# A decoder block on one core: the first products in a written order, two elementwise steps on other engines

## The chip, the core and the metric

The kernel runs on one core of one Trainium2 chip. Its engines are TensorE (PE in the profile; PEld is its loading of weights), VectorE (DVE), ScalarE (ACT), GpSimd (POOL) and SyncE (SP, which issues the transfers here). Each has a queue of its own and works it off in order; they wait for each other by semaphores. The metric is the device time of one execution in microseconds (us), the median of several runs.

## What is computed

One layer of a hybrid decoder for 256 tokens of width 1024, in float32: a norm, one combined projection, attention and a gated scan (SSD) beside each other, a mixed output, and a second part (PEER) that scores 16384 single-neuron experts. With one block of 256 keys the attention is plain causal attention with slopes. Cut to what the change touches:

```python
h = rms_norm(x, norm1_g)
q, k, v, z, xbc, dt_raw, g_attn, g_ssd = split(h @ w_in)
q, k = rms_norm(q, q_norm_g), rms_norm(k, k_norm_g)
s = q @ k.T * 64 ** -0.5 - slopes * dist            # per head, causal
p = softmax(s)
attn = p @ v
xs, bm, cm = split(silu(conv(xbc)))
acum = cumsum(dt * -exp(a_log))
lmat = exp(where(causal, acum[t] - acum[s], -inf))  # per scan head
y = (cm @ bm.T * lmat) @ (xs * dt)                  # 8 groups of 4 scan heads
x = x + (sigmoid(g_attn) * (attn @ w_attn_o) + sigmoid(g_ssd) * (norm(y) @ w_ssd_o)) @ w_out
x = x + peer(rms_norm(x, norm2_g))
```

## The kernel before

**Products.** Every float32 matrix is split into a high part that TensorE can take in one pass (type fp32r) and the rest. A product is the sum of three: high x high (hh), the low part of the activations with the high part of the weights (lh), and high with low (hl). `hTh` and `hTl` are the parts of the normed, transposed activations, `wh` and `wl` those of the weights.

**Weights.** `load_raw` (line 110) loads tiles of 128 x 1024 floats, 512 KB each, into three buffers `wr`, in the order in which they are used; `ahead` (line 116) keeps five loads and three splits ahead of the product. A split is one copy on ScalarE (`wh`, line 128) and one subtraction for `wl`, on VectorE (line 138) or, for every third or fourth tile, on GpSimd (line 133). A buffer `wr` is free for the next load when `wl` is made.

**Stages.** For each of 8 groups g: the columns of q and k (`psqk`), of v for two groups (`psv`), of xs (`psxs`), of B and C (`psbc`), of z (`psz`). Each such product is 48 matmuls of 256 columns on two weight tiles. `product_N` (line 198) has tokens as rows, `product_T` (line 165) as columns. Between the matmuls `tick` (line 151) calls generators that emit the other work in small steps: `decay` once (it makes `dt`, line 344, with the product `psdt` of 24 matmuls and the small transposes `psdtn`), and for each group `attention` (line 424), `conv`, `zgate` and `ssd` (line 556). So the order of TensorE is that of the program's text from the first group on. Other engines' instructions are put in order by a scheduler from its own estimates; `K` (line 80) keeps an instruction in program order instead, and is used for the start alone.

**The start.** SP loads the first 128 rows of x, the gains, weight tile 0, the other 128 rows, and tiles 1 and 2. TensorE runs 13 products of zeros (`pz`, line 282). `norm_T` (line 238) is a generator for each half of the rows: `rnm` (mean square plus epsilon, VectorE), `rn` (power -0.5, GpSimd), `xn` (rows scaled, VectorE), four and four transposes to `ptx`, then `hTh` (ScalarE, line 267) and `hTl` (VectorE, line 271) in pieces of 128 columns. The squares of the first half are summed by ScalarE, those of the second by VectorE (line 294). The tuple `START` (line 30) says in which order the two halves and the first splits are emitted. The first psqk uses `product_half` with `late`, which sorts the terms of a weight tile by hh, lh, hl.

**In attention**, after the exponentials `p` and their sums, VectorE makes the reciprocals `rs` (line 481), GpSimd scales the rows of p with two instructions per head (line 483), TensorE transposes them (`pp`, line 488). **In ssd**, `seg` makes the exponents `e` (VectorE, lines 583 and 584), and `damp` (line 586) takes the exponential and multiplies it with the masked scores `cbm` to `m`: two of four on VectorE, two on GpSimd. TensorE multiplies m with xs (`py`, line 619); `y`, `yT` and `yl` are VectorE's steps behind it.

Of the kernel before, what the change touches and what calls it, by code (L numbers as in the profile page):

```python
# [9 lines left out]
F32 = mybir.dt.float32  # L10
# [19 lines left out]
START = (0, 1, 2, 0, 1, 2, 1)  # L30
# [31 lines left out]
def tile_hybrid_block(ctx: ExitStack, tc: tile.TileContext, x, n1g, wblk, wdt, qkg, cw, cb, dtb,  # L62
# [135 lines left out]
    def product_N(ps, xh, xl, late=False):  # L198

        w = natural_w()  # L200
        for tt in range(2):
            product_half(ps, tt, w, xh, xl, late)

    def rstd_of(pool, ss, n, inv, name):
# [3 lines left out]
        state["pow"] = nc.gpsimd.tensor_tensor(q, r, neghalf[:, :n], op=OP.pow)  # L208
# [8 lines left out]
    with tc.tile_pool(name="pa", bufs=1) as pa, ExitStack() as ctx2:  # L217
# [20 lines left out]
        def norm_T(pool, tt, ss, gain, dh, dl, tag, row=False):  # L238
# [3 lines left out]
            if row and tt == 0:  # L242
                yield
            t = slice(128 * tt, 128 * tt + 128)
            pts = []
            for f in range(2):
                xn = pool.tile([128, 512], F32, name="xn", tag="w512", bufs=W512)
                c = slice(512 * f, 512 * f + 512)
                if row:
                    state["xn"] = V.scalar_tensor_tensor(xn, xt[:, tt, c], r, gain[:, c], op0=OP.mult, op1=OP.mult)  # L250
                else:
                    K(V.tensor_scalar(xn, xt[:, tt, c], r, None, op0=OP.mult))
# [5 lines left out]
            for f in range(2):  # L258
                if row:
                    k = slice(4 * f, 4 * f + 4)  # L260
                    state["behind"] = (
                        A.activation(dh[:, k, t], pts[f], AF.Copy),
                        V.tensor_tensor(dl[:, k, t], pts[f], f32(dh[:, k, t]), op=OP.subtract))
                else:
                    for c in range(4):
                        k = 4 * f + c
                        K(A.activation(dh[:, k, t], pts[f][:, c], AF.Copy, scale=gain[:, k:k + 1]))
                    for c in range(4):
                        k = 4 * f + c
                        state["behind"] = K(  # L270
                            V.scalar_tensor_tensor(dl[:, k, t], pts[f][:, c], gain[:, k:k + 1], f32(dh[:, k, t]),
                                                   op0=OP.mult, op1=OP.subtract))
                yield
# [7 lines left out]
        for _ in range(NWARM):  # L281
            mm(pz, zb[:, :128], zb, start=True, stop=True)

        ss1 = pa.tile([128, 2], F32, name="ss1")
        c0 = norm_T(wk, 0, ss1[:, 0:1], n1, hTh, hTl, "tr")
        c1 = norm_T(wk, 1, ss1[:, 1:2], n1, hTh, hTl, "at")
        sq = wk.tile([128, D], F32, name="sqx", tag="ar")
        K(A.activation(sq, xt[:, 0], AF.Square, accum_out=ss1[:, 0:1]))
        next(c0)
        state["cap"] = 1  # L290
        ahead()
        next(c0)
# [808 lines left out]
```

## Time and profile before

| what | value |
|---|---|
| median of 3 runs | 1246.58 us (1246.37 to 1247.64) |
| the profiled execution | 1246.86 us, its span (first to last instruction) 1244.8 us |
| busy in the span: TensorE, VectorE, ScalarE, GpSimd | 1228.4, 897.4, 633.9, 296.0 us |
| moved by DMA | 215 MB, 173 GB/s on the mean |
| chain that ended last, by engine | TensorE 90%, VectorE 6%, GpSimd 2% |

A page of the profile gives busy time by engine, the chain of work that ended last, and the costliest groups of instructions; the trace behind it can be asked for stretches, lines and waits. An average over the span mixes stages: attention and scan end near 310 us, and some 900 us of expert scoring follow. Matmuls overlap, so the time from start to start says more than the time of one. The granted clock of TensorE is given as a share of 2.4 GHz.

### The profile page before, as it was taken

To read this page: it belongs to the slowest core of one execution; us is meant where nothing else is said; L and a number is where in the kernel's file an instruction comes from. 1 tells how busy PE (TensorE), PEld (TensorE's weight loads), DVE (VectorE), ACT (ScalarE), POOL (GpSimd) and SP (SyncE) were. 2 spreads that over 40 slices of the span, in tenths; PEclk is the share of its full clock that TensorE was granted. 3 is DMA by queue.
4 is the path that set the end of the run, shared out by engine and by line. 5 is a ranking of instruction groups with operands and counts; after the bars stand their busy time and mean duration, and the time that the engine had idled before them with its cause. 6 is when DMAs were issued, how large, how long until landed. Compare 5 with 4: busy or idle time off the path is not lost.

```text
span 1244.8 us, 22716 instructions
## 1 busy us (share of the span) xinstructions
PE 1228.4 (99%) x9005; PEld 1140.7 (92%) x9005; DVE 897.4 (72%) x1583; ACT 633.9 (51%) x975; POOL 296.0 (24%) x160
## 2 busy tenths in 40 slices
PE   8999999999999999999999999999999999999998
PEld 6989989999999999999999999999988888888887
DVE  6888989899334566688697888999855555555554
ACT  5666666666434454554544544444445454444442
POOL 3355354444222122232323222222100000000000
PEclk8999999999999999999999999999999999999999
DMA  5434444444455464546555455444455555555553
GB/s 193 173 136 154 169 156 166 153 145 143 171 202 186 137 220 153 185 155 209 180 172 168 153 170 160 157 168 158 165 195 194 195 188 201 188 194 194 196 193 118
DMA packets 60345, 215.15 MB, mean 173 GB/s; under 512 B 7600, under 2 KB 8144, under 8 KB 60112
## 3 DMA queue, kind: packets, MB, share of 16 engines
q1 hardware_dynamic: 60240, 213.71, 50.3%
q8 instruction: 70, 1.15, 0.4%
q14 instruction: 35, 0.29, 0.1%
HBM read 212.60 MB, written 1.08 MB: 172 GB/s over the span
## 4 chain that ended last, share of the span: by engine, by line
PE 90%; DVE 6%; POOL 2%; issue 0%; DMA 0%; SPq 0%; ACT 0%; DVEq 0%; POOLq 0%
PE psu L933 10%; PE psu L935 10%; PE psu L934 10%; PE py L1020 9%; PE py L1022 9%; PE py L1021 9%; PE psqk L195 3%; PE psg L971 2%; PE psv L195 2%; PE psz L195 2%; PE pO L195 2%; POOL p L483 1%; DVE acc L538 1%; PE pS L175 1%; PE pS L176 1%; PE pS L174 1%
## 5 line engine op out<-in xcount | busy, mean ns | idle before, releaser
L128 ACT ACTIVATE wh<-wr 128x1024 fp32r<-128x1024 f32 x392 | 413.7, 1056 | 348.8 <-PE psu L934 96.2
L138 DVE TENSOR_TENSOR wl<-wr,wh 128x1024 fp32r<-128x1024 f32 x312 | 384.9, 1235 | 201.8 <-ACT wh L128 200.7
L133 POOL TENSOR_TENSOR wl<-wr,wh 128x1024 fp32r<-128x1024 f32 x79 | 204.0, 2583 | 421.4 <-ACT wh L128 355.3
L933 PE MATMUL psu<-xh,wh 128*128 128x256 f32 x1024 | 292.5, 286 | 0.0
L935 PE MATMUL psu<-xh,wl 128*128 128x256 f32 x1024 | 289.7, 283 | 0.0
L934 PE MATMUL psu<-xl,wh 128*128 128x256 f32 x1024 | 289.7, 283 | 0.0
L1020 PE MATMUL py<-wh,hh 128*128 128x512 f32 x512 | 199.2, 389 | 0.0
L1021 PE MATMUL py<-wl,hh 128*128 128x512 f32 x512 | 199.2, 389 | 0.0
L1022 PE MATMUL py<-wh,hl 128*128 128x512 f32 x512 | 199.2, 389 | 0.0
L934 PEld LDWEIGHTS psu<-xl,wh 128*128 128x128 f32 x1024 | 196.5, 192 | 0.0
L935 PEld LDWEIGHTS psu<-xh,wl 128*128 128x128 f32 x1024 | 196.3, 192 | 0.2 <-DVE wl L138 0.2
L933 PEld LDWEIGHTS psu<-xh,wh 128*128 128x128 f32 x1024 | 196.2, 192 | 0.0
L1022 PEld LDWEIGHTS py<-wh,hl 128*128 128x128 f32 x512 | 96.1, 188 | 20.1
L1021 PEld LDWEIGHTS py<-wl,hh 128*128 128x128 f32 x512 | 96.1, 188 | 19.9
L1020 PEld LDWEIGHTS py<-wh,hh 128*128 128x128 f32 x512 | 96.1, 188 | 19.8
L1012 ACT ACTIVATE hh<-gA 128x512 fp32r<-128x512 f32 x64 | 40.4, 632 | 88.8 <-PE py L1021 88.7
L1013 DVE SCALAR_TENSOR_TENSOR hl<-gA,hh 128x512 fp32r<-128x512 f32 x64 | 44.4, 693 | 52.3 <-ACT hh L1012 52.3
L958 DVE TENSOR_TENSOR og<-oh,g 128x1024 f16<-128x1024 f16 x64 | 58.5, 952 | 1.0
L538 DVE SCALAR_TENSOR_TENSOR acc<-u,cws,acc 128x254 f32<-128x254 f32 (+2 forms) x96 | 51.2, 566 | 0.5 <-ACT acc L534 0.4
L976 ACT ACTIVATE gA<-psg 128x24 f32<-128x24 f32 (+28 forms) x70 | 18.6, 281 | 64.4 <-DVE gA L974 55.2
L483 POOL TENSOR_SCALAR p<-p,rs 128x128 f32<-128x128 f32 (+1 forms) x32 | 41.1, 1298 | 38.5 <-DVE rs L481 38.5
L974 DVE TENSOR_TENSOR gA<-gA,psg 128x256 f32<-128x256 f32 (+12 forms) x120 | 38.1, 352 | 10.2 <-PE psg L971 9.8
(320 smaller groups left out, 2411.4 us busy)
## 6 DMA issues: line engine op xcount, KB each, us to landing
wr<-in_u_tab SPq DMA_DIRECT2D x128, 512.0 KB, 3.3
wr<-in_v_tab SPq DMA_DIRECT2D x128, 512.0 KB, 3.2
wr<-in_wblk SPq DMA_DIRECT2D x88, 512.0 KB, 3.3
wr<-in_wso SPq DMA_DIRECT2D x16, 512.0 KB, 4.1
wr<-in_wpq SPq DMA_DIRECT2D x16, 512.0 KB, 4.1
ar<-acT SPq DMA_DIRECT2D x8, 512.0 KB, 3.9
wr<-in_wao SPq DMA_DIRECT2D x8, 512.0 KB, 3.3
wr<-in_wou SPq DMA_DIRECT2D x8, 512.0 KB, 3.9
```

Of the source, the lines that this page charges most:

```text
L128: K(A.activation(h, r, AF.Copy))
L133: state["pool"] = nc.gpsimd.tensor_tensor(lo, r, f32(h), op=OP.subtract)
L138: state["wl"] = K(V.tensor_tensor(lo, r, f32(h), op=OP.subtract))
L195: mm(ps[:, tt], lhs[:, k, s], rhs, start=f == n == 0, stop=f == 1 and n == 11)
L538: V.scalar_tensor_tensor(acc[:, i, sh:], u[:, i, :T - sh], cws[:, ct, 3 - sh:4 - sh], acc[:, i, sh:], op0=OP.mult, op1=OP.add)
L933: mm(ps[:, jj], h[:, c], xh[:, c], start=c == 0, stop=False)
L934: mm(ps[:, jj], h[:, c], xl[:, c], start=False, stop=False)
L935: mm(ps[:, jj], lo[:, c], xh[:, c], start=False, stop=c == 7)
L958: V.tensor_tensor(og[:, i], oh[:, 1], g2[:, i, t].rearrange("p (g e) -> p g e", e=2)[:, :, None, :] .to_broadcast([128, 4, 128, 2]), op=OP ...
L1020: mm(o, hh[:, jj, s], h[:, c], start=j == 0, stop=False)
L1021: mm(o, hh[:, jj, s], lo[:, c], start=False, stop=False)
L1022: mm(o, hl[:, jj, s], h[:, c], start=False, stop=j == 127)
```

## The change

The start (norm, transposes, first splits and the first psqk) is no longer emitted by generators and `START`, but written out, each instruction with `K`, so that each engine has one given order. In it ScalarE sums the squares of both halves, VectorE makes hTh of the first half, ScalarE that of the second; GpSimd splits tile 0 in two halves and tile 1 after the second pair of xn; the two halves of psqk go to two PSUM tiles, with the products of the low part of tile 1 at the end; and `spin` puts products of zeros between. No `tick` runs in it, so `decay` comes 48 matmuls later against the products than before. SP issues the load of tile 3 before the eight small loads of constants, and tile 4 after them; psdt now stands inside psxs. Later, `scaled` goes from GpSimd to ScalarE, and all four `damp` to VectorE. The diff, cut:

```diff
-            if i == 0:
-                nc.gpsimd.tensor_tensor(lo[:, :512], r[:, :512], f32(h)[:, :512], op=OP.subtract)
-                state["rest"] = lo[:, 512:], r[:, 512:], f32(h)[:, 512:]
-            elif i in (1, 121) or (2 < i < n_u + 128 and not 116 <= i < 124 and i % (3 if i >= 88 else 4) == PS[i >= 88]):
+            if i == 121 or (2 < i < n_u + 128 and not 116 <= i < 124 and i % (3 if i >= 88 else 4) == PS[i >= 88]):
...
+        def spin(n):
+            for _ in range(n):
+                K(mm(pz, zb[:, :128], zb, start=True, stop=True))
...
+        def high(pt, tt, f):
+            t = slice(128 * tt, 128 * tt + 128)
+            for c in range(4):
+                k = 4 * f + c
+                if tt == 0:
+                    K(V.tensor_scalar(hTh[:, k, t], pt[:, c], n1[:, k:k + 1], None, op0=OP.mult))
+                else:
+                    state["high"] = K(A.activation(hTh[:, k, t], pt[:, c], AF.Copy, scale=n1[:, k:k + 1]))
...
+        def terms(tt, f, i, first=False, last=False):
+
+            h, lo = parts[f]
+            for c in range(4):
+                n = slice(256 * c, 256 * c + 256)
+                lhs, rhs = ((hTh, h), (hTh, lo), (hTl, h))[i]
+                K(mm(psqk0[tt], lhs[:, 4 * f + c, 128 * tt:128 * tt + 128], rhs[:, n],
+                     start=first and c == 0, stop=last and c == 3))
+
+        while state["loaded"] < LOAD_AHEAD - 2:
+            load_raw()
+        squares(0)
+        xn0 = normed(0)
+        pt0 = [turned_x(xn, 0) for xn in xn0]
+        spin(5)
+        r0, h0, l0 = weight(0)
+        high(pt0[0], 0, 0)
+        low(pt0[0], 0, 0)
+        for c in range(2):
+            n = slice(512 * c, 512 * c + 512)
+            K(nc.gpsimd.tensor_tensor(l0[:, n], r0[:, n], f32(h0)[:, n], op=OP.subtract))
+        squares(1)
+        high(pt0[1], 0, 1)
+        low(pt0[1], 0, 1)
+        terms(0, 0, 0, first=True)
+        terms(0, 0, 2)
+        spin(2)
+        terms(0, 0, 1)
+        r1, h1, l1 = weight(1)
+        xn1 = normed(1)
+        state["pool"] = after(K(nc.gpsimd.tensor_tensor(l1, r1, f32(h1), op=OP.subtract)), state["xn"])
+        state["wl"] = state["pool"]
+        spin(2)
+        terms(0, 1, 0)
+        pt1 = [turned_x(xn1[0], 1)]
+        terms(0, 1, 2)
+        pt1.append(turned_x(xn1[1], 1))
+        for f in range(2):
+            high(pt1[f], 1, f)
+            low(pt1[f], 1, f)
+            spin(2 - 2 * f)
+            terms(1, f, 0, first=f == 0)
+            terms(1, f, 2)
+            if f == 0:
+                terms(1, 0, 1)
+        terms(0, 1, 1, last=True)
+        terms(1, 1, 1, last=True)
...
-                    nc.gpsimd.tensor_scalar(p[hh][:, c], p[hh][:, c], rs[:, tt:tt + 1], None, op0=OP.mult)
+                    A.activation(p[hh][:, c], p[hh][:, c], AF.Copy, scale=rs[:, tt:tt + 1])
...
-                (V if r % 2 else nc.gpsimd).tensor_tensor(ms[r], e, cbm, op=OP.mult)
+                V.tensor_tensor(ms[r], e, cbm, op=OP.mult)
```

TensorE at the start, before: `ptx` are the transposes, `wh_120` and `wl_121` weight tile 0, `wh_167` and `wl_168` tile 1.

```order
L255 MATMUL ptx<-ident,xn 128x128 x8
L195 MATMUL psqk_229<-wh_120,hTh 128x256 x4
L195 MATMUL psqk_229<-wh_120,hTl 128x256 x4
L195 MATMUL psqk_229<-wl_121,hTh 128x256 x3
L255 MATMUL ptx<-ident,xn 128x128 x8
L195 MATMUL psqk_229<-wl_121,hTh 128x256
L195 MATMUL psqk_229<-wh_167,hTh 128x256 x4
L195 MATMUL psqk_229<-wh_167,hTl 128x256 x4
L195 MATMUL psqk_229<-wl_168,hTh 128x256 x4
```

The same place now, from the second group of transposes of the second half on: tile 0 is `wh_137` and `wl_138`, tile 1 `wh_174` and `wl_175`, the halves of psqk are `psqk_106` and `psqk_107`.

```order
L330 MATMUL psqk_106<-wh_174,hTl 128x256 x4
L294 MATMUL ptx<-ident,xn 128x128 x4
L270 LDWEIGHTS zb
L270 MATMUL pz<-zb 128x512
L270 LDWEIGHTS zb
L270 MATMUL pz<-zb 128x512
L330 MATMUL psqk_107<-wh_137,hTh 128x256 x4
L330 MATMUL psqk_107<-wh_137,hTl 128x256 x4
L330 MATMUL psqk_107<-wl_138,hTh 128x256 x4
L330 MATMUL psqk_107<-wh_174,hTh 128x256 x4
L330 MATMUL psqk_107<-wh_174,hTl 128x256 x4
L330 MATMUL psqk_106<-wl_175,hTh 128x256 x4
```

The transposes of the second half now stand between groups of products, with products of zeros behind them, and the eight products of the low part of tile 1 moved to the end of psqk.

VectorE at the start, before:

```order
L252 TENSOR_SCALAR xn<-xt,rn 128x512 x2
L294 SCALAR_TENSOR_TENSOR sqx,ss_105<-xt 128x1024
L206 TENSOR_SCALAR rnm<-ss_105 128x1
L271 SCALAR_TENSOR_TENSOR hTl<-ptx,n_82,hTh 128x128 x4
L252 TENSOR_SCALAR xn<-xt,rn 128x512 x2
L271 SCALAR_TENSOR_TENSOR hTl<-ptx,n_82,hTh 128x128 x4
```

And now:

```order
L287 TENSOR_SCALAR xn<-xt,rn 128x512 x2
L302 TENSOR_SCALAR hTh<-ptx,n_82 128x128 x4
L310 SCALAR_TENSOR_TENSOR hTl<-ptx,n_82,hTh 128x128 x4
L302 TENSOR_SCALAR hTh<-ptx,n_82 128x128 x4
L310 SCALAR_TENSOR_TENSOR hTl<-ptx,n_82,hTh 128x128 x4
L203 TENSOR_SCALAR rnm<-ss_105 128x1
L287 TENSOR_SCALAR xn<-xt,rn 128x512 x2
L310 SCALAR_TENSOR_TENSOR hTl<-ptx,n_82,hTh 128x128 x8
L134 TENSOR_TENSOR wl_261<-wr_110,wh_260 128x1024
L134 TENSOR_TENSOR wl_265<-wr_252,wh_264 128x1024
```

The squares left VectorE, eight hTh came to it, and all sixteen tiles of the first half stand ahead of the second rnm; the splits of tiles 2 and 3 follow hTl directly.

ScalarE in the attention of the fifth group, before (`p` is first the exponential, with its sums):

```order
L476 ACTIVATE p,sums<-s,mx 128x128
L476 ACTIVATE p,sums<-s,mx 128x256
L128 ACTIVATE wh_2464<-wr_2347 128x1024
L476 ACTIVATE p,sums<-s,mx 128x128
L476 ACTIVATE p,sums<-s,mx 128x256
L656 ACTIVATE yh<-pty,sg 128x256 x2
```

And now:

```order
L546 ACTIVATE p,sums<-s,mx 128x128
L546 ACTIVATE p,sums<-s,mx 128x256
L127 ACTIVATE wh_2478<-wr_2361 128x1024
L546 ACTIVATE p,sums<-s,mx 128x128
L553 ACTIVATE p<-p,rs 128x128
L553 ACTIVATE p<-p,rs 128x256
L546 ACTIVATE p,sums<-s,mx 128x256
```

The scaling of the first head stands between the two exponentials of the second.

## Rows read from the trace of the kernel before

**Rows 1.** The page: engines (busy us, share, instructions), transfers (KB each, us to landing)
```profile
PE 1228.4 (99%) x9005; PEld 1140.7 (92%) x9005; DVE 897.4 (72%) x1583; ACT 633.9 (51%) x975; POOL 296.0 (24%) x160
...
wr<-in_wblk SPq DMA_DIRECT2D x88, 512.0 KB, 3.3
```
**Rows 2.** Stretches: length, busy us and instructions by engine, granted clock, DMA share, GB/s
```profile
6.40:13.20 6.80, 3.97 (x21) 2.59 (x19) 4.95 (x10) 4.47 (x11) 3.14 (x4) 1.00 0.65 248
13.20:20.00 6.80, 5.46 (x24) 5.06 (x25) 6.80 (x16) 4.17 (x10) 3.61 (x5) 0.50 0.53 161
20.00:31.65 11.65, 11.65 (x99) 11.27 (x97) 6.79 (x17) 4.87 (x8) 4.19 (x2) 1.00 0.54 181
40.00:300.00 260.00, 254.42 (x2078) 236.82 (x2078) 232.40 (x433) 167.37 (x331) 124.26 (x79) 1.00 0.45 154
```
**Rows 3.** Timeline of VectorE at the start: start us, us, instruction [idle before <- ended by]
```profile
6.16 0.88 DVE L252 TENSOR_SCALAR xn<-xt,rn 128x512 f32<-128x512 f32 x2 [0.67 <-POOL rn L208]
...
11.19 1.13 DVE L271 SCALAR_TENSOR_TENSOR hTl<-ptx,n,hTh 128x128 fp32r<-128x128 f32 x4
12.23 3.67 DVE L252 TENSOR_SCALAR xn<-xt,rn 128x512 f32<-128x512 f32 x2
...
18.45 1.21 DVE L138 TENSOR_TENSOR wl<-wr,wh 128x1024 fp32r<-128x1024 f32 x1
```
**Rows 4.** Timeline of GpSimd at the start
```profile
11.33 0.56 POOL L208 TENSOR_TENSOR rn<-rnm,neghalf 128x1 f32<-128x1 f32 x1 [1.36 <-DVE rnm L206]
...
13.08 2.54 POOL L133 TENSOR_TENSOR wl<-wr,wh 128x1024 fp32r<-128x1024 f32 x1
```
**Rows 5.** Timeline of TensorE at the start
```profile
1.35 5.44 PE L282 MATMUL pz<-zb 128*128 128x512 f16 x13 [1.35 <-DVE zb L279]
6.71 1.09 PE L255 MATMUL ptx<-ident,xn 128*128 128x128 f32 x8
...
17.94 1.05 PE L195 MATMUL psqk<-wh,hTl 128*128 128x256 f32 x4
18.79 1.05 PE L195 MATMUL psqk<-wl,hTh 128*128 128x256 f32 x4
...
31.65 0.28 PE L174 MATMUL psxs<-hTh,wh 128*128 128x256 f32 x1
```
**Rows 6.** Whom TensorE waited for, 40 to 330 us: total us, times, longest
```profile
PE pty L651 <- DVE y L646: 1.5, 2, 1.2
PE pp L488 <- POOL p L483: 1.2, 2, 1.0
PE pp L488 <- DVE yl L660: 1.2, 1, 1.2
PE ptq L445 <- DVE qn L439: 0.9, 1, 0.9
PE py L619 <- POOL m L590: 0.4, 1, 0.4
```
**Rows 7.** Timeline of ScalarE at the start
```profile
7.57 1.06 ACT L128 ACTIVATE wh<-wr 128x1024 fp32r<-128x1024 f32 x1 [2.27 <-DMA wr<-in_wblk]
...
14.65 1.14 ACT L267 ACTIVATE hTh<-ptx,n 128x128 fp32r<-128x128 f32 x4 [2.13 <-PE ptx L255]
```
**Rows 8.** Timeline of GpSimd, 115 to 121 us
```profile
116.03 4.91 POOL L483 TENSOR_SCALAR p<-p,rs 128x128 f32<-128x128 f32 x4 [6.58 <-DVE rs L481]
```
**Rows 9.** Groups of VectorE: xcount | busy us, mean ns | idle before, releaser
```profile
L590 DVE TENSOR_TENSOR m<-e,cbm 128x384 f32<-128x384 f32 x16 | 13.9, 868 | 0.8 <-ACT e L588 0.7
```
**Rows 10.** Timeline of VectorE at three later places
```profile
119.66 1.50 DVE L538 SCALAR_TENSOR_TENSOR acc<-u,cws,acc 128x255 f32<-128x255 f32 x3 [0.22 <-ACT acc L534]
...
208.40 2.88 DVE L439 TENSOR_TENSOR qn<-qs,rqk 128x512 f32<-128x512 f32 x1 [0.53 <-POOL rqk L208]
...
237.10 0.54 DVE L590 TENSOR_TENSOR m<-e,cbm 128x384 f32<-128x384 f32 x1
```
**Rows 11.** Timeline of TensorE in the sixth group's second py
```profile
238.26 0.87 PE L619 MATMUL py<-m,xdt 128*64 128x256 f32 x8
```

More of the change, by code (lines that the diff above doesn't have):

```diff
@@ L29 @@
 NWARM = 13
-START = (0, 1, 2, 0, 1, 2, 1)
 PS = (1, 2)
@@ L196, in product_half, with product_N, half @@
             tick()
-    def product_N(ps, xh, xl, late=False):
+    def product_N(ps, xh, xl):
         w = natural_w()
         for tt in range(2):
-            product_half(ps, tt, w, xh, xl, late)
+            product_half(ps, tt, w, xh, xl)
+    def half(t):
+        return t.rearrange("p (a n) -> p a n", a=2)
     def rstd_of(pool, ss, n, inv, name):
@@ L236, in row, with norm_T @@
             return t
-        def norm_T(pool, tt, ss, gain, dh, dl, tag, row=False):
+        def norm_T(pool, tt, ss, gain, dh, dl, tag):
             r = rstd_of(pool, ss, 1, 1.0 / D, "rn")
             yield
-            if row and tt == 0:
+            if tt == 0:
                 yield
@@ L258, in norm_T @@
             for f in range(2):
[L259 to L272, printed above, removed]
+                k = slice(4 * f, 4 * f + 4)
+                state["behind"] = (
+                    A.activation(dh[:, k, t], pts[f], AF.Copy),
+                    V.tensor_tensor(dl[:, k, t], pts[f], f32(dh[:, k, t]), op=OP.subtract))
                 yield
@@ L281, in tile_hybrid_block @@
         for _ in range(NWARM):
-            mm(pz, zb[:, :128], zb, start=True, stop=True)
+            K(mm(pz, zb[:, :128], zb, start=True, stop=True))
+        def spin(n):
+            for _ in range(n):
+                K(mm(pz, zb[:, :128], zb, start=True, stop=True))
         ss1 = pa.tile([128, 2], F32, name="ss1")
-        c0 = norm_T(wk, 0, ss1[:, 0:1], n1, hTh, hTl, "tr")
-        c1 = norm_T(wk, 1, ss1[:, 1:2], n1, hTh, hTl, "at")
-        sq = wk.tile([128, D], F32, name="sqx", tag="ar")
@@ L304, in tile_hybrid_block, with squares, normed @@
-        del state["cap"]
+        psqk0 = [ps_tile("mm", f"psqk0{tt}")[:, :256] for tt in range(2)]
+        w0 = []
+        def squares(tt):
+            sq = wk.tile([128, D], F32, name="sqx", tag="ar")
+            K(A.activation(sq, xt[:, tt], AF.Square, accum_out=ss1[:, tt:tt + 1]))
+        def normed(tt):
+            r = rstd_of(wk, ss1[:, tt:tt + 1], 1, 1.0 / D, "rn")
+            xs = []
+            for f in range(2):
+                xn = wk.tile([128, 512], F32, name="xn", tag="w512", bufs=W512)
+                state["xn"] = K(V.tensor_scalar(xn, xt[:, tt, 512 * f:512 * f + 512], r, None, op0=OP.mult))
+                xs.append(xn)
+            return xs
@@ new lines, in low, with weight @@
+        def low(pt, tt, f):
+            t = slice(128 * tt, 128 * tt + 128)
+            for c in range(4):
+                k = 4 * f + c
+                state["behind"] = K(V.scalar_tensor_tensor(
+                    hTl[:, k, t], pt[:, c], n1[:, k:k + 1], f32(hTh[:, k, t]), op0=OP.mult, op1=OP.subtract))
+        def weight(i):
+            r = raw.pop(i)
+            h = ring.tile([128, 1024], F32R, name=f"wh{i}", tag="wh")
+            lo = ring.tile([128, 1024], F32R, name=f"wl{i}", tag="wl")
+            K(A.activation(h, r, AF.Copy))
+            parts[i] = (h, lo)
+            state["split"] = i + 1
+            state["next"] = i + 1
+            return r, h, lo
@@ new lines, in terms @@
+        def terms(tt, f, i, first=False, last=False):
+            h, lo = parts[f]
+            for c in range(4):
+                n = slice(256 * c, 256 * c + 256)
[6 more added lines that the diff above has]
+        xn0 = normed(0)
@@ new lines, in tile_hybrid_block @@
+        xn1 = normed(1)
[6 more added lines that the diff above has]
+        pt1.append(turned_x(xn1[1], 1))
+        for f in range(2):
+            high(pt1[f], 1, f)
[5 more added lines that the diff above has]
+                terms(1, 0, 1)
@@ L674, in tile_hybrid_block @@
         for g in range(NG):
-            ps = ps_tile("mm", f"psqk{g}")
-            product_N(half(ps), hTh, hTl, g == 0)
+            ps = psqk0
+            if g > 0:
+                ps = [ps_tile("mm", f"psqk{g}")]
+                product_N(half(ps[0]), hTh, hTl)
             held["qk", g] = ps
```

55 lines of the change are left out of this document (22 added, 33 removed).

## The prediction

> **What bounds the kernel now.** The page first: TensorE is busy for 99% of the span [rows 1]. Later work is a dense row of products, so time is won only where TensorE stands idle, runs slowly, or waits. The second view is the table by stretches [rows 2]. From 6.4 to 13.2 us TensorE has only 21 matmuls and is busy 3.97 of 6.80 us. From 13.2 to 20.0 us its granted clock is 0.50, so 1.2 GHz and not 2.4 GHz. From 20.0 us on it is dense at full clock: 99 matmuls in 11.65 us, 0.118 us each; I use 0.12. Then 40 to 300 us, the stage of attention and scan: TensorE busy 254.4 of 260, VectorE 232.4 of 260, ScalarE 167.4.
>
> The third view, the timelines of the start, says why. VectorE's two xn of the second half of x take 3.67 us from 12.23 on, where their first pair took 0.88 [rows 3]. Ahead of them stand the squares of that half, on VectorE too, and GpSimd's power, 11.33 to 11.89; beside them runs GpSimd's split of weight tile 1, 13.08 to 15.62 [rows 4]. The last four transposes can't start before 15.9, and TensorE, idle so long, has lost its clock by then: four products take 0.85 us from start to start (17.94 to 18.79), 0.213 each [rows 5]. The first product of psxs starts at 31.65; up to it TensorE has done psqk (48 products), psv (48), psdt (24) and two small transposes. I measure the start of both kernels there.
>
> The fourth view is who TensorE waits for from 40 to 330 us: 5.2 us in all, 1.2 for p scaled by GpSimd, 0.4 for m made by GpSimd, 3.6 for tiles of VectorE [rows 6].
>
> **The start, step by step.** Until the eight first transposes, 6.71 to 7.80 [rows 5], nothing changes. The new order then fixes each engine.
> 1. ScalarE splits tile 0 from 7.57 to 8.63, as before [rows 7], and takes the squares of the second half from VectorE; they are done before step 3 needs them, as each is one pass over 1024 columns like the split.
> 2. VectorE makes 16 small tiles, hTh and hTl of the first half, 7.4 on. Four hTl take 1.13 us with their tail, 0.263 each in sequence [rows 3]; VectorE's hTh has no row, and I take the same, as it too reads PSUM and writes 128 columns. 16 x 0.263 = 4.2, so 11.6. Bounds for the eight hTh: 0.20 each (the xn, 0.44 for 512 columns, shows that VectorE can be quicker per column) and 0.34 (no overlap between them): 0.5 us earlier to 0.6 later.
> 3. rnm 0.15, power 0.56, and the xn at 12.46, done at 12.95 and 13.35. GpSimd's split of tile 1 is made to wait for them, so the stretch to 3.67 is gone: the second xn is done 2.5 us earlier than now (15.9).
> 4. TensorE in its written order: four transposes 12.95 to 13.4 (eight took 1.09), four products (0.48), four transposes (0.44), two products of zeros. The 13 of the start took 5.44 us, 0.42 each for 512 columns [rows 5], twice the 0.213 of 256 columns at half clock; at full clock I take 0.21, and 0.42 as upper bound. So 14.75. The other nine zeros stand where TensorE would wait for ScalarE, VectorE or GpSimd anyway; without that cover each costs 0.21.
> 5. ScalarE's hTh of the second half: 1.14 per four [rows 7], 13.6 to 14.75 and on to 15.75. VectorE's hTl waits for all four of a half, so 14.8 to 15.9 and on to 16.95.
> 6. Products of the second half: hh from 14.75, lh with the last hTl at 15.9, then five more groups of four: 16.05 + 20 x 0.12 = 18.45. The two groups that need GpSimd's split of tile 1 stand last: 13.35 + 2.54 = 15.9, needed at 17.5, so it is hidden.
> 7. psv: VectorE's split of tile 2 follows hTl: 16.95 + 1.21 = 18.15, just in time; tile 3 at 19.4, needed at 20. Its load is issued when GpSimd frees the first buffer, about 11.3, and lands 3.3 us later [rows 1]. 48 products: 24.2.
> SP has the eight small loads behind that tile now, and ScalarE's split of tile 4 stands ahead of its copies of psqk; both have some 4 us before a matmul needs them (psdt now stands inside psxs), so I price them at nothing; without that cover TensorE would wait 1 to 2 us.
> Before, psxs began at 31.65 with psdt and the transposes done; less those 26 x 0.118 = 3.1 that is 28.55. **Start: 28.55 - 24.2 = 4.4 us earlier**, 3.7 to 4.9 by the bounds, if the clock holds.
>
> **The stage of attention and scan.** TensorE's order is unchanged here beyond the first group; other engines' tiles come at other times.
> - p: GpSimd loses 32 instructions; four take 4.91 us [rows 8]. ScalarE gets them; its instructions of 128 columns take 0.28 in sequence and of 1024 columns 1.06 [rows 7], so I take 0.35 and 0.45 for 128 and 256 columns, 16 x 0.8 = 13 us, in 93 us that it stands idle there. Behind an instruction that waits for the reciprocal rs stand the next exponentials and weight splits; the reciprocal is VectorE's next but one after the maxima for which ScalarE waits already, so half a us at most per head, and splits are made two tiles ahead. p is ready some 1.5 us sooner; I take the 1.2 us of waits as gone (bounds 0 and 1.2).
> - m: VectorE gets 16 more. One takes 0.87 on average now [rows 9], but 0.54 at 237.10, where nothing holds it up [rows 10]. So + 16 x 0.54 = 8.6 and - 16 x 0.33 = 5.3 on the old ones: + 3.4 us for VectorE in the whole stage, out of 27.6 idle. Cost to TensorE zero, gain the 0.4 of its wait.
> - The 3.6 us for VectorE's tiles I leave as they are: they come where VectorE is held up by a weight split on GpSimd (one qn took 2.88 us [rows 10], and TensorE's 0.9 for qn is its wait behind it [rows 6]), and the splits stay.
> Sum: **1.6 us**, and by the rivals below from -7.4 to +5.2.
> On GpSimd's p the trace shows more: three acc on VectorE, with two inputs from SBUF, took 1.50 us, 0.5 each as ever [rows 10], beside the p that ran from 116.03 to 120.94 [rows 8]. So taking p off GpSimd frees GpSimd, not VectorE. The Trainium skill (GPSIMD Engine Reference, Key points) says that GpSimd shares its SBUF interfaces with VectorE and contends with VectorE instructions in a 2-port mode or with two SBUF inputs; by that rule p would hold up acc too, and its removal would give VectorE time back. For the split beside xn the trace agrees with that page; for p it does not.
>
> Total 4.4 + 1.6 = 6.0. The profiled execution took 1246.86 us (span 1244.8), 0.3 above the median of 1246.58, so the difference is taken from either: 1246.58 - 6.0 = **1240.6 us**.
>
> **The rivals.**
> - The zeros don't hold the clock. For: it fell after a stretch with 3.97 us of work in 6.8, and nothing here shows zeros among products. Against: the filled order leaves TensorE idle only about 1.5 us there, and the clock that the first products had came after 13 products of zeros alone. Then, from 13.2 to 20.0 again at half clock: two times four transposes and one group of lh at the price of four products, 0.85 each, zeros 0.85, so 16.3; 17 of the 28 products until 20.0 at 0.213, eleven after it at 0.12: 21.3 instead of 18.45. Gain 1.5 + 1.6, 1243.5 us.
> - VectorE becomes the bound at py, and the time ends on the other side. Place: the second py of each group follows the last m by little: m ended at 237.64 [rows 10], py began at 238.26 [rows 11], so 0.6 us are spare, while two more m put 1.1 in the queue. If the 0.33 per m doesn't come back, TensorE waits 0.5 in each of eight groups, 4.0, and the 0.4 stays: 1246.6 - 4.4 - 1.2 + 4.0 = 1245.0. If the lag also passes on to y, yl and qn behind, it is the full 16 x 0.54 = 8.6: 1249.6, slower. It decides at 5.6, the 4.4 and 1.2 together. Against: VectorE idles 27.6 us in this stage.
> - All five waits vanish, since GpSimd, with less to do, starts its splits at once and holds VectorE up where nobody waits; VectorE gets its stretched time back. 1246.6 - 4.4 - 5.2 = 1237.0. The Trainium skill's rule cited above would lead here. For it: m's stretch. Against: the splits, which cause the long ones, stay.
>
> **How the numbers follow.** Forecast 60%; its own bounds are a start of 3.7 to 4.9 and waits of 0.3 to 2.9 (the last with half of VectorE's gone too), so 1238.8 to 1242.6. Clock lost 15%, 1243.5. VectorE late 12% in its small form, 1245.0, and 6% in its large one, 1249.6. All waits gone 7%, 1237.0. The range takes in the forecast, the lost clock and the nearer part of the third and last: 1237.8 to 1245.2. A measurement of this kernel tells some 0.2% (2.5 us) from no change, so faster means below 1244.1: 60 + 7 + 12 of the 15 = 0.79; same 3 + 12 = 0.15; slower 0.06.
>
> **What would show it.** Right: granted clock 1.00 in all of 6.4 to 31 us, the second xn done near 13.4, the last psqk product near 18.5, psxs near 24.2, and no waits for p or m. Wrong: a stretch at clock 0.50 between 13 and 20 us; TensorE waiting in the middle of psv for a weight split; py or pty waiting for VectorE in most groups; more waits for ScalarE's wh.

## The result, and the profile after

The changed kernel takes 1240.70 us (1239.60 to 1241.31) against 1246.58 us, a ratio of 0.9950 with an interval of 0.9938 to 0.9961. The forecast was 1240.6 us. The profiled execution of after took 1239.60 us (span 1237.8); its span is 7.0 us below that of before, a little more than the 5.9 us between the medians.

The time is met, but not by the way that the sum takes. The forecast gives 4.4 us to the start and 1.6 us to the stage of attention and scan. Done alone, the start brings 0.9 us (which can't be told from nothing) and the stage's two moves 4.4 us. Both terms were mis-sized, and the errors cancel: that the total is right is luck.

First the page and the table by stretches of after, which answer to [rows 1, 2]. Columns of a stretch are: length, busy us and instructions of TensorE, its weight loads, VectorE, ScalarE and GpSimd, granted clock, DMA share, GB/s.

```profile
PE 1225.8 (99%) x9016; PEld 1139.8 (92%) x9016; DVE 888.8 (72%) x1605; ACT 642.0 (52%) x1003; POOL 234.9 (19%) x112
```
```profile
6.40:13.20 6.80, 5.82 (x38) 4.41 (x38) 5.70 (x21) 3.27 (x4) 3.08 (x3) 1.00 0.64 247
13.20:20.00 6.80, 6.80 (x55) 6.42 (x53) 4.42 (x10) 4.78 (x12) 2.38 (x1) 1.00 0.59 185
...
40.00:300.00 260.00, 255.66 (x2099) 238.75 (x2098) 227.17 (x461) 179.32 (x367) 65.10 (x31) 0.99 0.46 155
53.00:56.50 3.50, 3.50 (x19) 2.86 (x19) 0.42 (x1) 0.76 (x2) 1.15 (x1) 0.52 0.61 219
```

The start is as forecast: 55 instructions of TensorE from 13.2 to 20.0 us where there were 24, at full clock. VectorE makes 22 instructions more in the whole kernel and is still busy 8.6 us less. The new thing is the last line. Just after 53 us the clock is at half, which it never was there before.

The timeline of VectorE in the start of after, which answers to [rows 3]:

```profile
9.36 1.12 DVE L302 TENSOR_SCALAR hTh<-ptx,n 128x128 fp32r<-128x128 f32 x4
10.39 1.12 DVE L310 SCALAR_TENSOR_TENSOR hTl<-ptx,n,hTh 128x128 fp32r<-128x128 f32 x4
...
12.23 0.88 DVE L287 TENSOR_SCALAR xn<-xt,rn 128x512 f32<-128x512 f32 x2 [0.67 <-POOL rn L205]
```

And TensorE there, which answers to [rows 5]:

```profile
14.43 0.82 PE L330 MATMUL psqk<-wh,hTh 128*128 128x256 f32 x4
...
18.43 0.28 PE L189 MATMUL psv<-wh,hTh 128*128 128x256 f32 x1
...
24.19 0.28 PE L170 MATMUL psxs<-hTh,wh 128*128 128x256 f32 x1
```

Whom TensorE waits for from 40 to 330 us in after, which answers to [rows 6] (total us, times, longest):

```profile
PE pscum L478 <- DVE av L473: 2.4, 1, 2.4
PE pty L721 <- DVE y L716: 1.1, 2, 0.6
PE ptx L640 <- ACT pT L562: 0.4, 1, 0.4
PE pp L558 <- ACT p L553: 0.2, 1, 0.2
```

Of the five waits of [rows 6] only the one for y is left. Four are gone, where the forecast had two go. Against that stand two small waits for tiles of ScalarE (0.4 and 0.2 us) and a large one that before did not have: 2.4 us for av, the last tile of the decay's chain. It is followed by the half clock of the table above.

To see where time comes and goes I compare the start of the same product in two traces, at three places that all kernels have in the same order of work: the first product of psbc in group 0 (38.78 us before), the first psxs in group 2 (102.78) and the first pA (341.50). The lead over before is:

| kernel | at psbc 0 | at psxs 2 | at pA | from psxs 2 to pA |
|---|---|---|---|---|
| after | 4.27 | 2.59 | 6.76 | +4.17 |
| e2, the stage's two moves alone | 0.89 | 1.45 | 5.45 | +4.00 |
| e3, the start alone | 3.77 | 0.17 | 0.13 | 0.0 |
| e8, rows alone | 0.02 | 0.26 | 1.06 | +0.80 |
| e11, decays alone | -0.15 | 1.81 | 2.33 | +0.52 |
| e4, after with pscum later | 3.91 | 3.98 | 8.36 | +4.38 |

The start's gain of some 4 us is there at 39 us and mostly spent by 103 us. Where both moves are made, they win their 4 us behind that. One trace is one execution, though: e2's start is the same program as that of before, so its 0.89 us at 39 us is chance, and the one new start put the first psxs at 24.19 to 24.68 us in five traces (after, e3, e4, e10, e12). This table is the frame of what follows.

### The profile page after: what moved, and what is told of

The parts are those of the page before. It is cut to its first block, busy times and chain, and to the rows that moved or that the text cites. A ratio compares the mean times of both kernels' runs of the same rounds, so it can differ in the third digit from the quotient of the medians.

```text
span 1237.8 us, 22707 instructions
## 1 busy us (share of the span) xinstructions
PE 1225.8 (99%) x9016; PEld 1139.8 (92%) x9016; DVE 888.8 (72%) x1605; ACT 642.0 (52%) x1003; POOL 234.9 (19%) x112
## 4 chain that ended last, share of the span: by engine, by line
PE 91%; DVE 5%; issue 1%; ACT 1%; POOL 1%; DVEq 0%; POOLq 0%
PE psu L1005 10%; PE psu L1007 10%; PE psu L1006 10%; PE py L1092 9%; PE py L1094 9%; PE py L1093 9%; PE psqk L189 3%; PE psz L189 2%; PE psg L1043 2%; PE pO L189 1%; PE psv L189 1%; PE psg L170 1%; PE pS L171 1%; PE psg L172 1%; PE psg L171 1%
## 5 line engine op out<-in xcount | busy, mean ns | idle before, releaser
L129 POOL TENSOR_TENSOR wl<-wr,wh 128x1024 fp32r<-128x1024 f32 x78 | 201.2, 2579 | 525.4 <-ACT wh L127 438.9
L1093 PEld LDWEIGHTS py<-wl,hh 128*128 128x128 f32 x512 | 96.1, 188 | 19.9
L608 DVE SCALAR_TENSOR_TENSOR acc<-u,cws,acc 128x254 f32<-128x254 f32 (+2 forms) x96 | 46.4, 514 | 3.2 <-ACT acc L604 3.2
L1025 DVE TENSOR_TENSOR oh<-iot,selT 128x2048 f16<-128x2048 f16 x32 | 38.9, 1215 | 2.7 <-PE psg L1043 2.7
```

What stands on the lines that cost most here:

```text
L129: state["pool"] = nc.gpsimd.tensor_tensor(lo, r, f32(h), op=OP.subtract)
L608: V.scalar_tensor_tensor(acc[:, i, sh:], u[:, i, :T - sh], cws[:, ct, 3 - sh:4 - sh], acc[:, i, sh:], op0=OP.mult, op1=OP.add)
L1093: mm(o, hh[:, jj, s], lo[:, c], start=False, stop=False)
```

## Experiments

The times are medians, each beside the kernel before as timed on the same chip. The ratio and its interval are made from all executions, so the ratio can differ a little from the quotient of the two medians; where they differ, go by the interval:

| kernel | us | before | ratio (95%) |
|---|---|---|---|
| after | 1240.70 | 1246.58 | 0.9950 (0.9938 to 0.9961) |
| e1 after, no zeros in gaps | 1240.55 | 1246.64 | 0.9955 (0.9941 to 0.9968) |
| e2 stage's moves alone | 1242.28 | 1246.64 | 0.9973 (0.9962 to 0.9983) |
| e3 start alone | 1245.74 | 1246.64 | 0.9997 (0.9988 to 1.0006) |
| e4 after, pscum later | 1238.16 | 1246.64 | 0.9938 (0.9925 to 0.9952) |
| e5 after, decay ahead | 1243.62 | 1246.91 | 0.9979 (0.9969 to 0.9990) |
| e6 start alone, decay ahead | 1253.24 | 1246.91 | 1.0051 (1.0038 to 1.0065) |
| e7 e5 without zeros | 1244.25 | 1246.91 | 0.9981 (0.9972 to 0.9990) |
| e8 rows alone | 1245.75 | 1246.91 | 0.9991 (0.9982 to 1.0000) |
| e9 e4 without zeros | 1238.48 | 1246.80 | 0.9936 (0.9922 to 0.9949) |
| e10 start alone, pscum later | 1244.30 | 1246.80 | 0.9979 (0.9970 to 0.9988) |
| e11 decays alone | 1244.20 | 1246.80 | 0.9982 (0.9973 to 0.9991) |
| e12 e4, tile 5 on VectorE | 1237.81 | 1246.80 | 0.9930 (0.9917 to 0.9944) |

### The two terms apart: e2 and e3

e2 is the kernel before with only these lines changed; e3 is after with the same lines put back.

```diff
-                    nc.gpsimd.tensor_scalar(p[hh][:, c], p[hh][:, c], rs[:, tt:tt + 1], None, op0=OP.mult)
+                    A.activation(p[hh][:, c], p[hh][:, c], AF.Copy, scale=rs[:, tt:tt + 1])
...
-                (V if r % 2 else nc.gpsimd).tensor_tensor(ms[r], e, cbm, op=OP.mult)
+                V.tensor_tensor(ms[r], e, cbm, op=OP.mult)
```

> The kernel before with its old start, and with only the two moves in the attention and scan stage: softmax rows scaled by ScalarE, all masked decays made by VectorE. The prediction's sum gives these two moves 1.6 us (waits for p 1.2 us and for m 0.4 us gone, the 3.6 us of waits for VectorE as they were): 1245.0 us, and waits for y, yl and qn still 3 to 4 us. Rival (from the trace after, where about 5 us are won between 57 and 330 us): the VectorE waits shrink too, to about 1 us, and the time is 1241.5 to 1243.0 us. Second rival: m on VectorE makes it late at py, and the time is 1246.6 or more.

> The changed kernel with its new start, and with the softmax rows and every second masked decay back on GpSimd as before. The prediction's sum gives the start 4.4 us: 1242.2 us. Rival (from the trace after, where TensorE waits 2.36 us for av at 51.39 us and then runs 3.41 us at half clock): the start wins 4.3 us by 24 us, gives about 4 of them (2.36 and half of 3.41) back by 57 us, and the time is 1244 to 1246 us; the wait for av of 2 to 2.5 us and a granted clock of 0.5 near 53 us are in its trace.

Measured: 1242.28 us for the stage's moves (4.4 us won by the medians, 2.1 to 4.7 by the interval) and 1245.74 us for the start (0.9 us, which can't be told from nothing). Both times lie in the rival's range, and the prediction's sum falls. But the waits that e2's rival named don't shrink to about 1 us. TensorE's waits from 40 to 330 us in e2:

```profile
PE pty L651 <- DVE y L646: 1.5, 2, 1.2
PE ptq L445 <- DVE qn L439: 1.0, 1, 1.0
PE ptx L570 <- ACT pT L492: 0.4, 1, 0.4
```

That is 2.9 us where before had 5.2, so this list tells only about half of the gain. TensorE has the same 9005 instructions in the same order in e2 as in before, so the lead can be followed from start to start. It grows by 1.2 us at the p near 51 us, by 1.6 where before waits for yl near 159 and by 0.9 at the qn near 211, falls by 1.1 at a qn near 72, and else changes in steps of under 0.6 us.

In the trace of e3 the lead of 3.77 us at 39 us is down to 0.17 us at 103 us. Some of that goes into waits for p on GpSimd, as the waits of TensorE from 30 to 100 us in e3 show:

```profile
PE pp L558 <- POOL p L553: 3.2, 2, 2.6
PE sc L532 <- ACT qkT L520: 1.3, 1, 1.3
...
```

So the rival's place was wrong in part. It expected the wait for av, and in e3 GpSimd's p comes first. Whoever comes first, TensorE stands there and the clock is down (0.95 on the mean from 31.65 to 50 us).

### What takes the start's gain in after: e4, e10, e12

The chain of the decay (the products psdt and psdtn, the dte tiles on VectorE, av, and the product pscum that sums av up along the tokens) is worked off in steps. product_half makes a step after every 12 products. The first psqk was made by product_N before and gave the chain four steps; written out by hand it gives none. So psdt now stands inside psxs, at 25.63 us and not at 24.12. Behind it VectorE is full. Two timelines of VectorE in after show the head and the end of the chain:

```profile
25.10 2.88 DVE L509 TENSOR_TENSOR qn<-qs,rqk 128x512 f32<-128x512 f32 x1 [1.76 <-POOL rqk L205]
27.95 0.47 DVE L425 CAST dist<-di 128x384 f32<-128x384 int32 x1
...
33.14 0.21 DVE L451 TENSOR_TENSOR dte<-psdtn,dtbr 128x64 f32<-128x64 f32 x1
...
51.12 0.21 DVE L473 SCALAR_TENSOR_TENSOR av<-dte,alr 128x64 f32<-128x64 f32 x1
```

The same tile in before:

```profile
46.03 0.22 DVE L405 SCALAR_TENSOR_TENSOR av<-dte,alr 128x64 f32<-128x64 f32 x1
```

av comes 5.1 us later, in a kernel whose products run 4.3 us earlier. TensorE meets it in the second psqk of after:

```profile
48.75 0.28 PE L189 MATMUL psqk<-wh,hTl 128*128 128x256 f32 x1
51.39 0.41 PE L478 MATMUL pscum<-av,mask 128*128 128x32 f32 x2 [2.36 <-DVE av L473]
...
54.65 0.41 PE L189 MATMUL psqk<-wl,hTh 128*128 128x256 f32 x1
54.86 0.42 PE L189 MATMUL psqk<-wh,hTl 128*128 128x256 f32 x1
```

The bracket is the wait. After it the products are 0.21 us apart and not 0.12: the half clock. e4 puts pscum two steps further on:

```diff
+            yield
+            yield
             pc = ps_tile("at", "pscum")
```

> The changed kernel with the two small cumulative products (pscum, pscumT) put two steps, 24 matmuls or some 2.9 us, further on in TensorE's order, so that av is done when they come. Theory (the wait of 2.36 us for av and the half clock of 3.41 us behind it cost 2.36 + 1.7 = 4.1 us of the end): no wait for av over 0.3 us, the clock stays at 1.00 after 6.4 us, and the time is 1236.2 to 1238.5 us. Rival: what is lost there is made up by later waits in any case, as the decays that the scan needs come no earlier: 1240.2 to 1241.2 us, with waits of 2 us or more that are new in 55 to 120 us.

Measured: 1238.16 us, 2.5 us below after. Two kernels below, e9 and e12, have the same edit; 14 of the 15 executions of the three are below the fastest of after (1239.60 us). There is no wait for av, and the clock is full:

```profile
50.00:60.00 10.00, 10.00 (x86) 9.76 (x85) 5.87 (x11) 6.66 (x11) 4.24 (x2) 1.00 0.58 187
60.00:95.00 35.00, 31.27 (x254) 28.65 (x253) 31.22 (x65) 21.95 (x48) 5.64 (x3) 1.00 0.48 160
```

The theory holds in kind and in the range that it gave, but the rival has a part of it. At the first psxs of group 1 the trace of e4 is 4.57 us ahead of that of after (55.47 us against 60.04), a little more than the 4.1 us expected for the wait and the half clock; at the next psxs, of group 2, it is 1.40 us. So of the 4.1 us 2.5 come in the time, since behind 60 us new waits are there (TensorE is busy only 31.27 of 35 us). The waits of e4 from 40 to 330 us:

```profile
PE ptn L702 <- DVE yT L696: 2.2, 1, 2.2
PE pp L560 <- DVE y L708: 1.1, 1, 1.1
PE py L691 <- DVE m L662: 0.4, 1, 0.4
PE ptx L642 <- ACT pT L564: 0.4, 1, 0.4
```

Against e2 (1242.28) the start is now worth 4.1 us, nearly what the prediction gave it. It was earned in the start and given away at the decay. (A later pscum without the new start was not tried; in e2 TensorE does not wait for av.)

e10 does the same to e3, the start alone. The edit is e3's and e4's together.

> The new start alone (rows and every second masked decay on GpSimd) with pscum two steps further on. Theory (it is the early pscum, with the half clock behind it, that took the start's gain: 1245.74 us with it): 1242.0 to 1243.0 us, the prediction's 4.4 us for the start nearly whole. Rival (GpSimd's rows, which are late at pp by 2.6 us near 45 us, take it in any case): 1244.5 to 1246 us with waits for p of 2 us or more.

Measured: 1244.30 us, 2.5 us below before, between the theory and the rival. The start brings 1.6 us more than in e3; the rest still goes to GpSimd, with waits for p of 2.3 us and for m of 1.1 us in the trace. With rows and decays on GpSimd the start can't be kept whole.

e12 asks whether the decay's chain still sets the time in e4. It is e4, and takes GpSimd's weight split away that stands beside the first qn (2.88 us) and ahead of the iotas.

```diff
-            if i == 121 or (2 < i < n_u + 128 and ...
+            if i == 121 or (5 < i < n_u + 128 and ...
```

> The kernel with pscum two steps further on, and with the sixth weight tile (number 5) split on VectorE, not GpSimd: nothing of GpSimd's stands beside the first qn (2.88 us there) and the iotas come some 2.4 us sooner. Theory (the decay's chain is still what the first scan waits for): qn takes 0.7 us, av is ready 1 to 2.5 us sooner than 51.1 us, the waits for yT and y near 83 to 87 us (3.3 us together) shrink by 1 us or more, and the time is 1236.3 to 1237.3 us. Rival: VectorE is full from 30 to 50 us, and a split more on it gives the gain back: 1238.2 us within 0.5, or more.

Measured: 1237.81 us, the fastest kernel of the study, 2.9 us below after by the medians. Against e4 alone (0.35 us) the difference can't be told. qn takes 0.69 us as expected, but av only comes at 50.1 us and not at 50.9, and the waits for yT (2.2 us) and y (1.1 us) are as long as in e4. VectorE, busy 17.72 of 18.35 us from 31.65 to 50 us in both, gives the rest back, as the rival says.

### Sooner instead of later: e5 and e6

If the chain lost four steps, giving them back should do more than moving pscum away. e5 makes four steps ahead of the first psv, and puts e4's two in front of pscum; e6 is the same with rows and decays on GpSimd.

```diff
         active.append(decay())
+        for _ in range(4):
+            tick()
```

> The changed kernel with the decay's chain four steps ahead: its conversion of wd, its iotas, masks and product (psdt) are issued ahead of the first psv product, as in the kernel before, where the first psqk product made these four steps; pscum stands two steps further on in the chain, so that in TensorE's order it comes two steps sooner than in the changed kernel. Theory (the changed kernel lost most of what its start won because the decay's chain lost its four steps: av is ready at 51.3 us against 46.3 before, and the scan of the first group is late by as much): av ready at 43 to 46 us, no wait for pscum over 0.5 us, clock 1.00 after 6.4 us, the 4.3 us of the start still there at 100 us, and the time is 1235.0 to 1237.0 us. Rival 1: where the chain is issued does not matter, VectorE's load between 31 and 100 us sets when the scan ends; av is not ready before 49 us and the time is 1238 to 1241 us. Rival 2: the chain ahead of the splits makes psv or psxs wait, which starts over 0.5 us later than 24.2 us.

> The same with the softmax rows and every second masked decay back on GpSimd: the new start and the decay's chain ahead, nothing of the stage's moves. Theory (the start is worth its 4.3 us where the decay's chain is not held back): 1242.3 us, within 0.8. Rival (GpSimd's rows and decays and VectorE between 31 and 100 us give the start's gain back whatever the decay does): 1245 to 1246.5 us, as with the start alone (1245.74).

Measured: 1243.62 and 1253.24 us, slower than after and, for e6, than before; e6 lies outside the ranges of its theory and of its rival. The first half of the theory is true: in e5 av is ready at 44.6 us, and nothing waits for it. But the start is lost at once. The timeline of TensorE in e5:

```profile
21.96 0.30 PE L438 MATMUL psdt<-hTh,wdh 128*32 128x256 f32 x1 [1.76 <-ACT qs L502]
```

By the code, the written-out psqk fills two of the three PSUM tiles that psdt shares with it, one for each half of the rows, and psv the third. So psdt waits until ScalarE has copied psqk out. This is rival 2 by another cause. The lead at 39 us is 2.12 us, and by 103 us it is -0.32 us. TensorE waits 2.3 us for m and 1.8 us for pT on the way, though av is early. In e6 it waits 3.6 us for p and then works from 50 to 60 us at a mean clock of 0.56; later it waits 3.4 us for y, and its lead at 103 us is -7.84 us. So an early av is not enough, and my theory that the decay alone holds the scan back falls. Why the order in which VectorE takes its work from 60 to 95 us comes out worse in e5 than in e4, I did not settle.

### The stage's moves apart: e8 and e11

e8 has only the first pair of the diff of e2, e11 only the second.

> The kernel before with one move alone: softmax rows scaled by ScalarE; masked decays as before, every second one on GpSimd. The two moves together gave 1242.28 against 1246.64 us. The prediction's sum has 1.2 us for p and 0.4 us for m, so three quarters of what the two bring are p's: if so, 1243.3 us, within 0.5. Rival 1: it is the decays, with which GpSimd held up VectorE and py: 1245.5 to 1246.6 us. Rival 2: the rows bring it all and m on VectorE costs something: 1242.2 us or less.

> The kernel before with one move alone: every masked decay on VectorE; the rows still scaled by GpSimd. The rows alone gave 1245.75 against 1246.91, both moves 1242.28 against 1246.64. Theory (each move is worth its own: GpSimd's rqk starts right behind its m, and the waits for qn go with m): 3.0 to 3.5 us, 1243.4 to 1243.9 us, and the wait of 0.9 us for qn near 210 us is gone. Rival (only the two together free GpSimd in time; alone the rows still hold it): 1245.5 to 1246.9 us. Prediction's price for m alone: 0.4 us, 1246.4.

Measured: 1245.75 us for the rows (1.2 us, just what the prediction had for p, but expected here was 3.6; its interval reaches down to nothing) and 1244.20 us for the decays (2.6 us, less than the 3.0 to 3.5 of the theory; the prediction had 0.4). Together they bring 4.4. The lead table says more. From 103 to 341 us the rows win 0.80 us, the decays 0.52 us, both 4.00 to 4.38 us, in each of the three kernels of the table that have both. Of what the decays win alone, 1.96 us lie before 103 us, where both together win only 0.56 (1.45 less the 0.89 of chance). So the two don't add up place by place. The waits of TensorE from 95 to 330 us in e8:

```profile
PE ptq L445 <- DVE qn L439: 1.2, 2, 0.9
PE ptx L570 <- ACT pT L492: 0.4, 1, 0.4
PE py L619 <- DVE m L590: 0.2, 1, 0.2
```

And in e11:

```profile
PE pp L488 <- DVE yl L660: 1.2, 1, 1.2
PE ptq L445 <- DVE qn L439: 0.4, 1, 0.4
PE pp L488 <- POOL p L483: 0.2, 1, 0.2
```

Each move works on one wait that is written down to VectorE, and the other stays. The wait for yl goes with the rows: in before VectorE takes a weight split between the two yl (157.33 and 158.86), in after both yl come first (153.38, x2). The wait for qn near 211 us falls from 0.9 to 0.4 us with the decays, and only with both moves is it gone. qn needs rqk, a small power on GpSimd, and that needs rqk5m of VectorE. VectorE and GpSimd in before, then in e2:

```profile
203.35 1.82 DVE L138 TENSOR_TENSOR wl<-wr,wh 128x1024 fp32r<-128x1024 f32 x1
205.56 0.16 DVE L206 TENSOR_SCALAR rqk5m<-ss 128x8 f32<-128x8 f32 x1
205.80 2.57 POOL L208 TENSOR_TENSOR rqk<-rqk5m,neghalf 128x8 f32<-128x8 f32 x1 [1.71 <-DVE rqk5m L206]
```
```profile
200.77 0.17 DVE L206 TENSOR_SCALAR rqk5m<-ss 128x8 f32<-128x8 f32 x1
201.01 3.68 POOL L208 TENSOR_TENSOR rqk<-rqk5m,neghalf 128x8 f32<-128x8 f32 x1 [7.39 <-DVE rqk5m L206]
```

In before rqk5m stands behind a weight split of 1.82 us, which takes 1.22 alone; GpSimd makes an m beside it (203.07 to 204.08 us). In e2 and e11 all four m and rqk5m come ahead of that split: 4.8 us sooner in e2 (200.77), 3.5 in e11 (202.09), while the products were 2.7 and 1.8 us ahead.

Most of what the decays win alone comes earlier, and the prediction left it alone too: from start to start the lead of e11 grows by 0.5 us at the m near 71 us, by 1.1 at the y near 86 and by 0.5 at the qn near 211. TensorE's wait for y from 40 to 330 us is 1.5 us in before [rows 6]; in e11:

```profile
PE pty L651 <- DVE y L646: 0.4, 2, 0.3
```

Ahead of that y stands the qn of group 1. VectorE in before, then in e11:

```profile
69.84 1.50 DVE L439 TENSOR_TENSOR qn<-qs,rqk 128x512 f32<-128x512 f32 x1 [1.56 <-POOL rqk L208]
```
```profile
68.81 0.69 DVE L439 TENSOR_TENSOR qn<-qs,rqk 128x512 f32<-128x512 f32 x1
```

The idle time is gone, and y comes 1.8 us sooner (83.63 against 85.43 us). In e2 it is not gone: there VectorE waits 1.53 us for rqk, this qn takes 2.86 us, and the wait for y is 1.5 us as before.

And m on both engines at once costs VectorE. Its timeline in before, while GpSimd makes an m from 199.47 to 201.49 us, then in e2:

```profile
200.53 1.38 DVE L590 TENSOR_TENSOR m<-e,cbm 128x384 f32<-128x384 f32 x1
```
```profile
199.83 1.02 DVE L590 TENSOR_TENSOR m<-e,cbm 128x384 f32<-128x384 f32 x2
```

1.38 us for one beside GpSimd's, 0.5 each without. In e11 32 m take 19.9 us, where 16 took 13.9 [rows 9]: 6.0 us more. Yet from 95 to 330 us VectorE is busy 196.84 us in e11 and 200.48 in before. 13 m more there cost it less than nothing. In e8 it is 198.87 us.

### What the zeros are worth: e1, e7, e9

Each leaves out the products of zeros in the gaps (the 13 at the very start stay): e1 of after, e7 of e5, e9 of e4.

```diff
         def spin(n):
-            for _ in range(n):
-                K(mm(pz, zb[:, :128], zb, start=True, stop=True))
+            pass
```

> The changed kernel without the products of zeros in the gaps (the 13 at the very start stay). Theory (the zeros hold TensorE's granted clock): with them gone the clock falls to 0.5 somewhere between 8 and 20 us as it does in the kernel before (13.19 to 20.02 us there), the psxs product starts 2.3 to 3.4 us later than the 24.19 us of the changed kernel, and the time is 1243.0 to 1244.1 us. Rival 1: the new order alone keeps the clock; psxs still starts within 0.3 us of 24.2 and the time is 1240.7 within 0.5. Rival 2: the zeros stand in the way of products that could run; psxs starts earlier than 24.0 us and the time is 1239.5 to 1240.4.

> The kernel with the decay ahead, without the products of zeros in the gaps. Theory (the zeros hold the granted clock): it falls to 0.5 between 12 and 20 us for 3 to 7 us, psxs starts 0.7 to 3 us later, and the time is 0.7 to 3 us above that of the kernel with the decay ahead and the zeros. Rival: what falls in the start is made up in the stage behind it, or the clock falls just as often with the zeros: within 0.5 us of it.

> The kernel with pscum two steps further on (1238.16 us), without the products of zeros in the gaps. There the start's gain is not lost to the wait for av, so that what the zeros are worth can come through. Theory (they hold the granted clock): it falls to 0.5 for 3 to 4 us between 12 and 17 us, psxs starts 0.5 to 1.0 us later, and the time is 1238.7 to 1239.3 us. Rival 1 (as the prediction priced it, 2.9 us): 1240.6 to 1241.5. Rival 2 (worth nothing): 1238.2 within 0.3.

Measured: 0.15 us less, 0.6 more and 0.3 more than with the zeros; none can be told from nothing. The clock does fall without them. The stretches of e1, then of e9:

```profile
6.40:13.20 6.80, 4.40 (x28) 3.31 (x27) 5.74 (x21) 3.27 (x4) 3.09 (x3) 0.98 0.64 240
13.20:20.00 6.80, 6.80 (x47) 6.80 (x46) 4.32 (x10) 4.69 (x12) 2.37 (x1) 0.77 0.55 156
```
```profile
6.40:13.20 6.80, 4.80 (x26) 3.86 (x27) 5.75 (x21) 3.27 (x4) 3.09 (x3) 0.86 0.71 254
13.20:20.00 6.80, 6.80 (x49) 6.54 (x48) 4.52 (x10) 5.01 (x12) 2.37 (x1) 0.89 0.56 162
```

With the zeros the clock is 1.00 in both stretches in all seven traces that have them, without them it is below 1.00 in all three (e7: 0.85 and 0.90). So they hold the clock, as the theory says. But psxs starts only 0.74 us later in e1 (24.93) and 0.19 us in e9 (24.72 against 24.53, within what the start varies), and in e1 even that is given back: a shorter half clock than the forecast's rival had, part of it where TensorE waits anyway.

## Why the prediction came out right, step by step

**The start, steps 1 to 7: right.** VectorE's hTh had no row; I took 0.263 each, and four take 1.12 us. The 16 tiles end at 11.51 (11.6 forecast), the second xn at 13.11 (13.35), the second half begins at 14.43 (14.75), psv at 18.43 (18.45), psxs at 24.19 (24.2). The granted clock is 1.00 throughout. One cover was short: TensorE waited 0.50 us for GpSimd's first split at 11.07, without effect.

**What the start is worth at the end: wrong.** The failed step is the sentence behind step 7: the small loads and ScalarE's copies of psqk have some 4 us before a matmul needs them, psdt now standing inside psxs, "so I price them at nothing". I looked at who comes next, not at the end of the decay's chain. av came 5.1 us late: 2.36 us of waiting, then half clock. The four steps that the chain lost are the main part of it (with them given back, in e5, av is 6.7 us sooner than in after); the qn of 2.88 us beside a split is 0.8 us of it at most (e12 against e4). With pscum out of the way the same start is worth 4.1 us (e4 against e2); as it is, 1.6 us (after against e2); alone 0.9 us. How far VectorE's work behind 60 us could have kept up in any case is open.

**Rows: right by number.** ScalarE takes 12.7 us for them (13 forecast), and alone they bring 1.2 us (1.2), which hardly can be told from nothing. That the numbers meet is partly luck: in the trace of e8 the lead grows by 1.2 us at the p near 51 us and by 1.6 where before waits for yl, a wait that I had left, and gives back 0.6 at GpSimd's m near 71 us and 1.0 at a qn near 241. They won part of their gain only with the decays.

**Decays: the mis-sized term.** Forecast: VectorE +3.4 us, gain 0.4. Measured alone: VectorE busy 894.9 us in the whole kernel against 897.4, gain 2.6. I took 0.33 us a piece off the 16 old m, and nothing off the rest. In the row [rows 10] for qn the releaser in the bracket, GpSimd's rqk, was the hint: a wait "for VectorE" that leads to GpSimd, and from there back to a rqk5m of VectorE behind a split that GpSimd's m drew out. "I leave as they are" was the wrong treatment of these 3.6 us: with the decays alone the wait for y shrinks by 1.1 us and that for qn by 0.5.

**The rivals.** The lost clock (zeros): without them the clock does fall, but the price was -0.15 to 0.6 us, not to be told from nothing, and not 2.9. VectorE late at py: no wait for m or py is in the list of after. All five waits gone: nearest to what happened in the stage (four of five in after, three in e2), and held at 7%. The Trainium skill (GPSIMD Engine Reference, Key points) led there: contention with instructions of VectorE that have two SBUF inputs. For m the measurement agrees (1.38 us beside GpSimd's m, 0.5 alone). For p it hardly does: the 22 acc that VectorE makes beside GpSimd's p in before take 0.52 us on the mean, those beside nothing of GpSimd's 0.47, so "as ever" in the prediction was nearly right. With only the rows gone VectorE is busy 1.6 us less from 95 to 330 us, and in the whole kernel no less (899.2 us against 897.4).

## What to carry to other kernels

A gain at the start is worth what the next meeting point leaves of it: when one engine's order moves by some us, follow every chain that the moved code used to step on, to its last tile, and not only to its first reader. A wait's releaser is where the chain last passed, not its cause; look one or two steps further, into the queue of whoever released that one, before leaving a wait "as it is". And test the terms of a sum one by one, because here two wrong terms made a right time.

## What the runs showed of the hardware

In after TensorE stood for 2.36 us from 49 us on, and the granted clock was 0.52 from 53.0 to 56.5 us; so in that trace one wait cost its own length and half of 3.5 us again. Without the products of zeros the clock of the start fell to 0.77 to 0.90 on the mean of 13.2 to 20.0 us (e1, e7, e9), and in the time that can't be measured. e9 had executions with a mean clock of 1.000 and of 0.997 that took 1238.46 and 1238.39 us; the record doesn't show where in them the clock was down. That TensorE waits for VectorE later on in any case is a likely reason, but was not tested apart. Two products of mask and decay at once on VectorE and GpSimd stretched VectorE's from 0.5 to 1.38 us, while GpSimd's scaling of rows, with one tensor as input, stretched VectorE's acc only from 0.47 to 0.52 us.
